# A fused decoder layer in program order on every engine: split stream, four-way decay, heads in pairs

## The chip, the cores and the metric

The kernel runs on one core of a Trainium2 chip. A core has a matrix engine (PE, TensorE), a vector engine (DVE), a scalar engine (ACT), a general engine (POOL) and a queue that issues transfers (SP); each runs its own instructions in order and waits on semaphores for the others. Tensors are read from HBM into on-chip memory (SBUF) by DMA; PE writes its results into PSUM, 128 partitions wide. The metric is the time of one execution in microseconds (us).

## The reference

One layer of a hybrid decoder, one sequence of 256 tokens, width 2048:

```python
h = rmsnorm(x, norm_gain[l])
z = h @ w_in[l]
(gq, gk_, gv, ggate, gdown, fq, fk, fv, flogit, fgate,
 mq, mgate, merge) = jnp.split(z, IN_OFFSETS, axis=-1)
gk_log = log_sigmoid(gdown @ w_gk_up[l] + b_gk[l]) / 16
o_a = gla_chunked(gq, gk_, gv, gk_log)      # S_t = diag(exp g_t) S_{t-1} + k_t v_t^T ; o_t = q_t S_t
o_a = rmsnorm(o_a, gla_norm_gain[l]) * silu(ggate)
log_f = log_sigmoid(flogit + b_f[l])
o_b = forgetting_attention(fq, fk, fv, log_f) * silu(fgate)   # causal, bias cumsum(log_f)
mk, mv = jnp.split(rmsnorm(mem, mem_norm_gain[l]) @ w_mem_kv[l], 2, axis=-1)
o_c = memory_attention(mq, mk, mv) * silu(mgate)
gates = sigmoid(merge.reshape(B, S, 3, D))
y = sum(gates[:, :, i] * (o_i @ wb_i) for i in range(3))
return rmsnorm(x + y @ w_out[l], final_gain)
```

Gated linear attention (GLA) has 4 heads (keys 128, values 256), the forgetting attention (fox) 8 heads of 64, the cross-attention 4 heads of 128 over 256 memory tokens. All inputs and outputs are 32-bit floats.

## The kernel before, in words

**Products.** Every wide product runs as split products: a 32-bit weight w is cast to a form that PE multiplies fast (`hi`, on ACT, L124) and the rest is kept as `lo = w - hi` (on DVE, L125). x and the memory are split likewise, with the norm's gain folded in (`split_x`; L256, L257). A product is then hi times hi, hi times lo and lo times hi. The weights come in blocks of 512 columns and 16 k-tiles ("kt", 128 rows each), as four quarters of 1 MB. A raw quarter lies in one of three `raw` buffers; it is split into two pieces of two kts, and there are four buffers each for `hi` and `lo`.

**Blocks.** A block runs either as `natural` (tokens on the partitions, weights moving: per kt and half of the tokens three 512-wide matmuls, L166 to L168) or as `transposed` (columns on the partitions, x moving: a 512-wide matmul with `hi`, which has x's hi and lo side by side, and a 256-wide one with `lo`, L187 and L189, for four groups of columns c and, after the first block, four kts at a time). In order of time: GLA queries (block 0, transposed), keys (1, transposed), values (2 and 3, natural), fox queries and keys (4 and 5, transposed), fox values (6), memory keys and values (7 and 8), memory queries (9), five gates, then four times three merge gates and one branch projection, then four output blocks.

**Side work.** The norm is applied late: sums of squares of x are taken on ACT, `rsqrt` makes `xcol`, and a matmul of ones with a diagonal of it makes `xrow` (`row_of`), by which results are scaled. A small product (L386, 16 matmuls) gives the low-rank decay input and the forget logits. The GLA decay is a running sum (L432) of log-sigmoids (L401 to L405). The scores inside a chunk of 128 are built in seven levels (block sizes 64 down to 1): per level DVE and ACT make scaled queries and keys, PE multiplies them for the eight chunk heads (64 columns each, L495), DVE multiplies by a mask (L497) and adds (L500); a diagonal term is added first (L477, L478). Fox handles a head in stages (scores L568, L569; masked maximum L571; exponents L576; normalising L580; transposes L585; values L593, L594). Side work stands in generators ("lanes"), and `pull()` runs one step of two lanes after each kt.

**What sets the order.** In this kernel PE and SP run in the order in which the program was written. DVE, ACT and POOL are ordered by the framework's scheduler; weight splits have a priority 1000 ahead of everything else. In block 0 the loads of x and weights come in small portions, interleaved with their splits.

**Names in the change.** `w_load`, `w_split`, `first_piece`: the new stream of loads and splits; `post`: a third lane for evictions; `small`, `rms_of`, `row_of`, `gla_decay`, `gla_scores`, `fox`, `memory`: the generators. In listings below a name such as `hi_264` is one tile, `raw_259<-wall` a load.

Of the kernel before, what the change touches and what calls it, by code (L numbers as in the profile page):

```python
# [51 lines left out]
AHEAD = 1000  # L52
LEVEL_GAP = 11
N_WARM = 8
LEVELS = (64, 32, 16, 8, 4, 2, 1)
# [4 lines left out]
def body(ctx, tc, xT, memT, xn, memn, wall, wsm, wup, cst, fgain, out):  # L60
# [7 lines left out]
    bpool = ctx.enter_context(tc.tile_pool(name="bpool", bufs=6))  # L68
# [4 lines left out]
    ctx.enter_context(tc.manual_schedule(engines={mybir.EngineType.PE, mybir.EngineType.SP}))  # L73
# [42 lines left out]
    main, side = Lane(), Lane()  # L116

    def pull():
        side.pull()
        main.pull()  # L120


    def split_w(src, hi, lo):
        nc.scalar.copy(hi, src)  # L124
        nc.vector.tensor_tensor(out=lo, in0=src, in1=hi.bitcast(F32), op=ALU.subtract)  # L125

    def w_quarter(i, q):
        raw = wpool.tile([P, 4, NB], F32, tag="raw", name=nm("raw"), bufs=3)
        nc.sync.dma_start(raw, wall[i, :, 4 * q:4 * q + 4, :])
        res = []  # L130
        for s in range(2):
            hi = wpool.tile([P, 2, NB], F32R, tag="hi", name=nm("hi"))
            lo = wpool.tile([P, 2, NB], F32R, tag="lo", name=nm("lo"))
            split_w(raw[:, 2 * s:2 * s + 2, :], hi, lo)
            res.append((hi, lo))
        return res
# [8 lines left out]
    def w_kts(i):  # L145

        for kt in range(KT):
            if kt % 4 == 0:
                with tc.high_priority(AHEAD):
                    res = w_quarter(i, kt // 4)  # L150
            hi, lo = res[(kt % 4) // 2]
            yield kt, hi[:, kt % 2, :], lo[:, kt % 2, :]
# [19 lines left out]
    def transposed(h, wsrc, bank=acc, group=4):  # L172
# [4 lines left out]
        ps = [bank() for _ in range(4)]  # L177
        held = []
        for item in wsrc:
# [3 lines left out]
            for c in range(4):  # L183
                cs_ = slice(c * P, (c + 1) * P)
                for kt, hi, lo in held:
                    hk = h_of(h, kt)
                    MM(ps[c], lhsT=hi[:, cs_], rhs=hk.rearrange("p a s -> p (a s)"),  # L187
                       start=(kt == 0), stop=False, skip_group_check=True)
                    MM(ps[c][:, :S], lhsT=lo[:, cs_], rhs=hk[:, 0, :], start=False,  # L189
                       stop=(kt == KT - 1), skip_group_check=True)  # L190
                if group == 4:
                    pull()
            for _ in held if group < 4 else ():
                pull()
            held = []
        return ps


    def rsqrt(r, m4, n):
# [4 lines left out]
        nc.scalar.activation(p, p, AF.Exp, scale=-0.5)  # L204
        nc.vector.tensor_tensor(out=u, in0=p, in1=p, op=ALU.mult)
# [3 lines left out]
    def rms_of(src, col, stage):  # L209

        ssq = spool.tile([P, NT, 2], F32, tag="ssq", name=nm("ssq"))
        for t in range(NT):
            for c in range(2):
                raw = stage()
                nc.sync.dma_start(raw, src[:, t, c * 1024:(c + 1) * 1024])
                nc.scalar.activation(raw, raw, AF.Square, accum_out=ssq[:, t, c:c + 1])
                yield 2
# [3 lines left out]
        rsqrt(col, ms, NT)  # L221
        yield 3

    def row_of(col, row):
# [4 lines left out]
        yield 3  # L229
        ps = att()  # L230
        MM(ps[:, :S], lhsT=ones, rhs=dg.rearrange("p t s -> p (t s)"), start=True, stop=True)
        nc.scalar.copy(row, ps[:, :S])
# [20 lines left out]
    x12 = []  # L253
# [5 lines left out]

    def load_split(src, tag, gcol, g, h, raw, ks):  # L260

        nc.sync.dma_start(raw[:, ks, :], src[:, 4 * g + ks.start:4 * g + ks.stop, :])
        for k in range(ks.start, ks.stop):
            kt = 4 * g + k
            split_x(h, raw[:, k, :], k, cs[:, gcol + kt:gcol + kt + 1])
# [6 lines left out]
    def load_mem():  # L272
        for g in range(4):
            m12.append(new_h("m12_", g))
            raw = wpool.tile([P, 4, S], F32, tag="raw", name=nm("raw"), bufs=3)
            load_split(memT, "m12_", C_MGAIN, g, m12[g], raw, slice(0, 4))
            yield 6

    def first_w():

        wb = w_block()
        for g in range(4):
            raw = wpool.tile([P, 4, NB], F32, tag="raw", name=nm("raw"), bufs=3)
            xraw = a4([P, 4, S])
            h = new_h("x12_", g)
            x12.append(h)
            step = 1 if g < 2 else 2
            for s in range(2):
                with tc.high_priority(AHEAD):
                    hi = wpool.tile([P, 2, NB], F32R, tag="hi", name=nm("hi"))  # L290
                    lo = wpool.tile([P, 2, NB], F32R, tag="lo", name=nm("lo"))
                    for k in range(0, 2, step):
                        ks = slice(2 * s + k, 2 * s + k + step)
                        load_split(xT, "x12_", C_GAIN, g, h, xraw, ks)
                        cut = (0, 256, NB) if g == 0 and ks.start == 0 else (0, NB)
                        for a, b in zip(cut, cut[1:]):
                            nc.sync.dma_start(raw[:, ks, a:b], wall[wb, :, 4 * g + ks.start:4 * g + ks.stop, a:b])
                            split_w(raw[:, ks, a:b], hi[:, k:k + step, a:b], lo[:, k:k + step, a:b])
                for k in range(2):
                    yield 4 * g + 2 * s + k, hi[:, k, :], lo[:, k, :]  # L300
# [8 lines left out]
    def plain_T(ps):  # L309

        r = a4([P, 4, S])
        for c in range(4):
            nc.scalar.copy(r[:, c, :], ps[c][:, S:])
            nc.vector.tensor_tensor(out=r[:, c, :], in0=ps[c][:, :S], in1=r[:, c, :], op=ALU.add)
        return r

    def scale_T(r, row):
        nc.vector.tensor_tensor(out=r, in0=r, in1=row.unsqueeze(1).to_broadcast([P, 4, S]), op=ALU.mult)
        return r

    def evac_T(ps, row):
        return scale_T(plain_T(ps), row)

    def evac_N(ps, col):
        r = a4([P, NT, NB])
        for t in range(NT):
            nc.scalar.activation(r[:, t, :], ps[t], AF.Copy, scale=col[:, t:t + 1])  # L327
        return r

    def proj_T():  # L330
        return evac_T(transposed(x12, w_kts(w_block())), xrow)

    def proj_N():
        return evac_N(natural(x12, range(KT), w_kts(w_block())), xcol)

    G["q"] = plain_T(transposed(x12, first_w(), att, 1))


    wsr = cpool.tile([P, KT, 24], F32, name="wsr")
    nc.sync.dma_start(wsr, wsm)  # L340
    wup_s = cpool.tile([16, 512], F32, name="wup_s")
    nc.sync.dma_start(wup_s, wup)

    gmask = cpool.tile([P, len(LEVELS), 64], F32, name="gmask")
    nc.gpsimd.memset(gmask, QS)
    for li, s in enumerate(LEVELS):
        nb = 64 // s
        mk_ = gmask[:, li, :].rearrange("p (b s) -> p b s", s=s)
        nc.gpsimd.affine_select(out=mk_, in_=mk_, pattern=[[-2 * s, nb], [0, s]],
                                compare_op=ALU.is_ge, fill=0.0, base=0, channel_multiplier=1)  # L350
        nc.gpsimd.affine_select(out=mk_, in_=mk_, pattern=[[2 * s, nb], [0, s]],
                                compare_op=ALU.is_ge, fill=0.0, base=s - 1, channel_multiplier=-1)
    gdiag = cpool.tile([P, P], F32, name="gdiag")
    nc.vector.tensor_scalar(gdiag, ident, QS, None, ALU.mult)

    fmask = cpool.tile([P, 3 * P], F32, name="fmask")
    nc.gpsimd.memset(fmask, 0.0)
    for c in (0, 2):
        nc.gpsimd.affine_select(out=fmask[:, c * P:(c + 1) * P], in_=fmask[:, c * P:(c + 1) * P],
                                pattern=[[-1, P]], compare_op=ALU.is_ge, fill=-1e30,  # L360
                                base=0, channel_multiplier=1)


    zs = []
    for g in range(2):
        z0 = a4([P, 8, P], F32)
        nc.gpsimd.memset(z0, 0.0)
        ws = a4([P, 8, P], F32R)
        wr = wsr[:, 8 * g:8 * g + 8, :]
        nc.vector.tensor_copy(ws, z0)  # L370
        for (a, b, wdt) in ((0, 0, 16), (32, 16, 8)):
            nc.vector.tensor_copy(ws[:, :, a:a + wdt], wr[:, :, b:b + wdt])
            nc.vector.tensor_tensor(out=ws[:, :, 64 + a:64 + a + wdt], in0=wr[:, :, b:b + wdt],
                                    in1=ws[:, :, a:a + wdt].bitcast(F32), op=ALU.subtract)
        zs.append(ws)
    sm = cpool.tile([64, S], F32, name="sm")

    def small_and_norm():

        yield 5  # L380
        norm = rms_of(xn, xcol, lambda: a4([P, 1024]))
        for _ in range(4):
            yield next(norm)
        sp = att()
        for kt in range(KT):
            MM(sp, lhsT=zs[kt // 8][:, kt % 8, :], rhs=h_of(x12, kt).rearrange("p a s -> p (a s)"),  # L386
               start=(kt == 0), stop=(kt == KT - 1))
# [541 lines left out]
```

## Time and profile before

| | |
|---|---|
| time, median of 3 runs | 824.92 us (824.08 to 825.22) |
| profiled execution, its own time | 824.89 us |
| its span, first to last instruction | 823.2 us |
| PE busy, DVE, ACT, POOL | 809.6, 497.6, 408.4, 15.4 us |
| mean granted clock of PE | 0.997 |
| bytes read from HBM | 154.39 MB |
| last matmul ends, execution ends | 814 us, 823 us |

Busy time of an engine is the sum of its instructions; matmuls are pipelined, so a row's duration is longer than the time between two starts, and the time that a matmul holds PE is read as the difference of two start times. In rows of groups the last numbers are the count, the busy time with the mean in ns of one, and the idle time just before the group with what ended it. In rows of time they are start, duration and what ran, with the idle time before it and its releaser in brackets.

### The profile page before, as it was taken

The page shows a single profiled execution, that of the slowest core. Times are in us where ns is not written, and L with a number is a line of the kernel's source. Part 1 is how long each engine was busy: PE and PEld are TensorE (multiplying, and loading weights), DVE is VectorE, ACT ScalarE, POOL GpSimd, SP SyncE. Part 2 cuts the span into 40 slices and gives each one's busy share as a digit, 9 for nine tenths or more (in the row PEclk, how much of TensorE's full clock was granted, in tenths as well). Part 3 has the DMA queues.
Part 4 walks back from the last instruction along what each step waited for, and adds up shares of the span by engine and source line. Part 5 has one row for each costly group of instructions (what it writes and reads, how often), then busy time and mean ns, then how long its engine had stood idle before and what let it go on. Part 6 is the DMA issues. An engine that isn't in the chain of part 4 may idle for free.

```text
span 823.2 us, 10033 instructions
## 1 busy us (share of the span) xinstructions
PE 809.6 (98%) x3958; PEld 679.4 (83%) x3958; DVE 497.6 (60%) x657; ACT 408.4 (50%) x547; POOL 15.4 (2%) x36
## 2 busy tenths in 40 slices
PE   8999999999999999999999999999999999999995
PEld 7888888888888778888888888888888888888885
DVE  6755988875647667567445744475446544566833
ACT  7746755743454456455444444444444444445611
POOL 4000100000000000000000000000000000000000
PEclk9999999999999999999999999999999999999998
DMA  8943466844534344445555545554555455576803
GB/s 302 385 176 125 155 228 230 300 158 169 189 140 168 108 148 154 148 160 199 182 187 199 205 170 192 200 204 167 191 205 202 166 195 205 199 266 249 307 0 103
DMA packets 27359, 157.15 MB, mean 191 GB/s; under 512 B 3216, under 2 KB 4640, under 8 KB 10416
## 3 DMA queue, kind: packets, MB, share of 16 engines
q1 hardware_dynamic: 27040, 156.48, 53.3%
q8 instruction: 31, 0.51, 0.2%
q14 instruction: 16, 0.13, 0.0%
q10 hardware_dynamic: 144, 0.02, 0.0%
q0 software_dynamic: 128, 0.02, 0.0%
HBM read 154.39 MB, written 2.10 MB: 190 GB/s over the span
## 4 chain that ended last, share of the span: by engine, by line
PE 90%; DVE 3%; DMA 2%; ACT 2%; issue 1%; SPq 1%; POOL 0%; DVEq 0%; ACTq 0%; POOLq 0%
PE acc L166 18%; PE acc L168 18%; PE acc L167 18%; PE acc L187 12%; PE acc L189 6%; PE acc L822 4%; PE acc L821 4%; PE acc L820 4%; DMA raw<-wall 1%; PE att L495 1%; DMA raw<-memT 1%; PE att L187 1%; DVE lo L125 1%; ACT hi L124 1%; PE att L593 1%
## 5 line engine op out<-in xcount | busy, mean ns | idle before, releaser
L125 DVE TENSOR_TENSOR lo<-raw,hi 128x1024 fp32r<-128x1024 f32 (+2 forms) x269 | 321.0, 1203 | 248.4 <-ACT hi L124 248.0
L124 ACT CAST hi<-raw 128x1024 fp32r<-128x1024 f32 (+2 forms) x269 | 275.3, 1035 | 291.1 <-PE acc L168 215.2
L166 PE MATMUL acc<-hi,x 128*128 128x512 f32 x544 | 215.3, 396 | 0.0
L168 PE MATMUL acc<-hi,x 128*128 128x512 f32 x544 | 212.0, 390 | 0.0
L167 PE MATMUL acc<-lo,x 128*128 128x512 f32 x544 | 211.8, 389 | 0.0
L187 PE MATMUL acc<-x,hi 128*128 128x512 f32 x384 | 137.2, 400 | 1.1 <-ACT a L327 1.1
L168 PEld LDWEIGHTS acc<-hi,x 128*128 128x128 f32 x544 | 102.1, 188 | 21.7
L166 PEld LDWEIGHTS acc<-hi,x 128*128 128x128 f32 x544 | 102.2, 188 | 21.2 <-issue 0.5
L167 PEld LDWEIGHTS acc<-lo,x 128*128 128x128 f32 x544 | 102.2, 188 | 20.5
L189 PE MATMUL acc<-x,lo 128*128 128x256 f32 x384 | 107.3, 280 | 0.0
L187 PEld LDWEIGHTS acc<-x,hi 128*128 128x128 f32 x384 | 72.1, 188 | 18.1 <-ACT a L327 1.6
L189 PEld LDWEIGHTS acc<-x,lo 128*128 128x128 f32 x384 | 72.4, 189 | 0.3
L166 PE MATMUL acc<-hi,oT 128*128 128x512 f32 x128 | 49.8, 389 | 0.0
L167 PE MATMUL acc<-lo,oT 128*128 128x512 f32 x128 | 49.8, 389 | 0.0
L168 PE MATMUL acc<-hi,oT 128*128 128x512 f32 x128 | 49.8, 389 | 0.0
L820 PE MATMUL acc<-hi,a 128*128 128x512 f32 x96 | 37.5, 391 | 0.0
L822 PE MATMUL acc<-hi,a 128*128 128x512 f32 x96 | 37.4, 389 | 0.0
L821 PE MATMUL acc<-lo,a 128*128 128x512 f32 x96 | 37.4, 389 | 0.0
L167 PEld LDWEIGHTS acc<-lo,oT 128*128 128x128 f32 x128 | 24.0, 188 | 5.0
L168 PEld LDWEIGHTS acc<-hi,oT 128*128 128x128 f32 x128 | 24.0, 188 | 5.0
L166 PEld LDWEIGHTS acc<-hi,oT 128*128 128x128 f32 x128 | 24.0, 188 | 5.0
L187 PE MATMUL att<-x,hi 128*128 128x512 f32 x64 | 23.4, 406 | 0.5 <-ACT hi L124 0.5
(215 smaller groups left out, 781.3 us busy)
## 6 DMA issues: line engine op xcount, KB each, us to landing
raw<-wall SPq DMA_DIRECT2D x132, 1024.0 KB, 4.7
a<-xn SPq DMA_DIRECT2D x8, 512.0 KB, 8.5
raw<-wall SPq DMA_DIRECT2D x4, 512.0 KB, 7.2
raw<-memT SPq DMA_DIRECT2D x4, 512.0 KB, 4.2
raw<-memn SPq DMA_DIRECT2D x4, 512.0 KB, 4.6
out<-a SPq DMA_DIRECT2D x8, 256.0 KB, 3.3
raw<-wall SPq DMA_DIRECT2D x7, 256.0 KB, 4.9
a<-xT SPq DMA_DIRECT2D x8, 128.0 KB, 4.2
```

What stands on the lines that cost most here:

```text
L124: nc.scalar.copy(hi, src)
L125: nc.vector.tensor_tensor(out=lo, in0=src, in1=hi.bitcast(F32), op=ALU.subtract)
L166: MM(ps[t], lhsT=h1, rhs=hi, start=(kt == first), stop=False)
L167: MM(ps[t], lhsT=h1, rhs=lo, start=False, stop=False)
L168: MM(ps[t], lhsT=h2, rhs=hi, start=False, stop=(kt == last))
L187: MM(ps[c], lhsT=hi[:, cs_], rhs=hk.rearrange("p a s -> p (a s)"), start=(kt == 0), stop=False, skip_group_check=True)
L189: MM(ps[c][:, :S], lhsT=lo[:, cs_], rhs=hk[:, 0, :], start=False, stop=(kt == KT - 1), skip_group_check=True)
L495: MM(ps[:, e, :], lhsT=E[:, e * P:(e + 1) * P], rhs=Q[:, e, :], start=True, stop=True)
L593: MM(o, lhsT=fv[:, 0, hs], rhs=pt[:, :S], start=True, stop=False, skip_group_check=True)
L820: MM(ps, lhsT=h1, rhs=hi, start=(kt == 0), stop=False)
L821: MM(ps, lhsT=h1, rhs=lo, start=False, stop=False)
L822: MM(ps, lhsT=h2, rhs=hi, start=False, stop=(kt == KT - 1))
```

## The change

1. All five engines now run in program order. What the scheduler decided on DVE, ACT and POOL is now where the generators stand.
2. The weights become one stream over all blocks but the last: `w_split(n)` splits piece n, `w_load` loads its quarter, and a block asks for pieces three ahead of the one it multiplies (`AHEAD = 3`). From the fourth quarter on `w_load` is asked for two quarters ahead. Block 0's pieces, which also load and split x, are made by `first_piece`.
3. Evictions (`join`, `proj_N`, gates) are steps of the lane `post`, and chains such as `rsqrt`, `log_sigmoid` and the silu gates have more `yield`s, that is, kts between their steps.
4. The small product (now L366) runs in three parts during block 0 and block 1; the memory's loads are staged in other buffers than `raw`, and the norms of x and memory load two halves at a time.
5. GLA scores: levels of 64 to 1 become three four-way levels (32, 8, 2; a block of 4s tokens against its three earlier quarters, 192 columns a matmul) and a level for pairs with the diagonal. Scores are copied under a mask into `gA` (`copy_predicated`, L636) in place of multiply and add. The term between the two chunks of 128 (L485 before, L582 now) is as it was.
6. Fox heads go in pairs, with the value matmuls of the two heads in turn on the two halves of the PSUM partitions. Memory heads are staged one step apart.
7. Warm-up matmuls 8 to 7; the small tiles' pool 6 to 8 buffers.

```diff
-AHEAD = 1000
+AHEAD = 3
+N_WARM = 7
+STEPS = (32, 8, 2)
-    ctx.enter_context(tc.manual_schedule(engines={mybir.EngineType.PE, mybir.EngineType.SP}))
+    ctx.enter_context(tc.manual_schedule())
...
     def pull():
+        post.pull()
         side.pull()
         main.pull()
...
+    def w_load(upto):
+        while done[0] <= min(upto, 4 * N_STREAM - 1):
+            i, q = divmod(done[0], 4)
+            raws[done[0]] = wpool.tile([P, 4, NB], F32, tag="raw", name=nm("raw"), bufs=3)
+            if i:
+                nc.sync.dma_start(raws[done[0]], wall[i, :, 4 * q:4 * q + 4, :])
+            done[0] += 1
+    def w_split(upto):
+        while done[1] <= min(upto, 8 * N_STREAM - 1):
+            n = done[1]
+            q, s = divmod(n, 2)
+            w_load(q + (2 if q >= 3 else 0))
+            hi = wpool.tile([P, 2, NB], F32R, tag="hi", name=nm("hi"))
+            lo = wpool.tile([P, 2, NB], F32R, tag="lo", name=nm("lo"))
+            if q < 4:
+                first_piece(q, s, raws[q], hi, lo)
+            else:
+                split_w(raws[q][:, 2 * s:2 * s + 2, :], hi, lo)
+            parts[n] = (hi, lo)
+            done[1] += 1
...
+    def small():
...
+        yield 2
+        nc.sync.dma_start(wsr, wsm)
+        nc.sync.dma_start(wup_s, wup)
+        yield 5
+        for g in range(2):
+            ws, wr = zs[g], wsr[:, 8 * g:8 * g + 8, :]
+            for (a, b, wdt) in ((0, 0, 16), (32, 16, 8)):
+                nc.vector.tensor_copy(ws[:, :, a:a + wdt], wr[:, :, b:b + wdt])
+                nc.vector.tensor_tensor(out=ws[:, :, 64 + a:64 + a + wdt], in0=wr[:, :, b:b + wdt],
+                                        in1=ws[:, :, a:a + wdt].bitcast(F32), op=ALU.subtract)
+            yield 1
+        sp = acc()
+        for kts, n in ((range(0, 8), 3), (range(8, 12), 4), (range(12, 16), 1)):
+            for kt in kts:
+                MM(sp, lhsT=zs[kt // 8][:, kt % 8, :], rhs=h_of(x12, kt).rearrange("p a s -> p (a s)"),
+                   start=(kt == 0), stop=(kt == KT - 1))
+            yield n
...
+            for c in range(4):
+                ps = att()[:, :2 * Q_N].rearrange("p (a b) -> p a b", a=2)
+                for j in range(2):
+                    e = 2 * c + j
+                    MM(ps[:, j, :], lhsT=E[:, e * P:(e + 1) * P], rhs=Qs[c // 2][:, e % 4, :],
+                       start=True, stop=True)
...
+                yield 1
+                for dst, mask, src in places:
+                    nc.vector.copy_predicated(
+                        dst, mask.bitcast(U32).unsqueeze(1).to_broadcast(list(src.shape)), src)
...
+        def values(p):
+            po = att()
+            for a, b, j, sl in ((0, S, 0, slice(0, S)), (P, S, 1, slice(S, 3 * P))):
+                for e in range(2):
+                    h = 2 * p + e
+                    MM(po[64 * e:64 * e + 64, a:b], lhsT=fv[:, j, h * 64:(h + 1) * 64], rhs=pts[h][:, sl],
+                       start=(j == 0), stop=(j == 1), skip_group_check=True)
+            return po
```

Three places show how the instructions moved. First the loads on SP in block 0: `xT` and `wall` into an `a` and a `raw` tile are x and weights, `wsr` and `wup_s` the small weights. Before, the loads of block 0's last quarter (`raw_291`) and the first of block 1 (`raw_406`, `raw_448`):

```order
L262 DMA a_237<-xT 128x512
L297 DMA raw_236<-wall 128x1024
L262 DMA a_292<-xT 128x512
L297 DMA raw_291<-wall 128x1024
L340 DMA wsr<-wsm 128x384
L342 DMA wup_s<-wup 16x512
L129 DMA raw_406<-wall 128x2048
L129 DMA raw_448<-wall 128x2048
```

and now, where the last quarter of block 0 is `raw_259` and block 1 begins with `raw_260` and `raw_262`:

```order
L353 DMA wsr<-wsm 128x384
L354 DMA wup_s<-wup 16x512
L328 DMA a_205<-xT 128x512
L331 DMA raw_202<-wall 128x1024
L144 DMA raw_260<-wall 128x2048
L144 DMA raw_262<-wall 128x2048
L328 DMA a_266<-xT 128x512
L331 DMA raw_259<-wall 128x1024
```

Block 1's two quarters moved ahead of block 0's last one, and the small weights ahead of its third one's second half.

Second, DVE in the same stretch, in the changed kernel: L300 and L132 are the splits of x and weights, L359 and L360 make the split small weights.

```order
L132 TENSOR_TENSOR lo_234<-raw_202,hi_233 128x1024
L300 SCALAR_TENSOR_TENSOR x_38_267<-a_266,cs,x_38_267 128x256 x2
L132 TENSOR_TENSOR lo_265<-raw_259,hi_264 128x1024
L359 CAST a_188<-wsr 128x8x16
L360 TENSOR_TENSOR a_188<-wsr,a_188 128x8x16
L359 CAST a_188<-wsr 128x8x8
L360 TENSOR_TENSOR a_188<-wsr,a_188 128x8x8
```

On PE the first eight small matmuls, which read `a_188`, now stand between kt 9 and kt 10 of block 0:

```order
L215 MATMUL att_183<-x_29_206,hi_203 128x512
L217 MATMUL att_183<-x_29_206,lo_204 128x256
L366 MATMUL acc_326<-x_7_113,a_188 128x512 x4
L366 MATMUL acc_326<-x_14_147,a_188 128x512 x4
L215 MATMUL att_174<-x_29_206,hi_233 128x512
```

Before, the 16 small matmuls stood together late in block 1, and the small weights were split on DVE when block 0 had ended.

Third, DVE around `xcol` (L244 to L246) and the diagonal for PE's L273, at the turn from block 1 to block 2, in the changed kernel:

```order
L132 TENSOR_TENSOR lo_648<-raw_539,hi_647 128x1024
L132 TENSOR_TENSOR lo_652<-raw_539,hi_651 128x1024
L300 SCALAR_TENSOR_TENSOR m_72_573<-a_574,cs,m_72_573 128x256
L244 TENSOR_TENSOR nwu_626<-nwp_625 128x2
L245 SCALAR_TENSOR_TENSOR nwu_626<-nwu_626,ms_622 128x2
L246 SCALAR_TENSOR_TENSOR xcol<-nwu_626,nwp_625 128x2
L270 TENSOR_SCALAR b_666<-ident,xcol 128x128 x2
```

In before the scheduler had put this chain among block 1's splits. On ACT the steps of the log-sigmoid (L457 to L462), the memory's splits (L299) and the weight casts (L131) stand in this order in block 2, up to the exponents of the cross-chunk term (L574, L575), which PE's L582 uses:

```order
L131 CAST hi_785<-raw_681 128x1024
L299 ACTIVATE m_94_702<-a_703,cs 128x256
L462 ACT_TABLE_LOAD
L462 ACTIVATE a_725<-a_725 128x1024
L462 ACTIVATE fc<-fc 8x256
L299 ACTIVATE m_94_702<-a_703,cs 128x256
L131 CAST hi_807<-raw_681 128x1024
L131 CAST hi_832<-raw_730 128x1024
L131 CAST hi_853<-raw_730 128x1024
L413 ACTIVATE a_850<-acc_643,xcol 128x512
L299 ACTIVATE m_113_817<-a_818,cs 128x256
L574 ACT_TABLE_LOAD
```

The casts of the weight stream stand in one queue with the chain's steps, where a priority had put them ahead before.

More of the change, by code (lines that the diff above doesn't have):

```diff
@@ L170, in natural, with transposed @@
         return ps
-    def transposed(h, wsrc, bank=acc, group=4):
-        ps = [bank() for _ in range(4)]
+    def transposed(h, wsrc, evac, bank=acc, group=4):
+        ps = [None] * 4
         held = []
@@ L195, in transposed, with last @@
             held = []
-        return ps
+        if group < 4:
+            for c in range(3):
+                evac(c, ps[c])
+        def last():
+            yield 1
+            evac(3, ps[3])
+        post.append(last())
     def rsqrt(r, m4, n):
@@ L274, in load_mem @@
             m12.append(new_h("m12_", g))
[L275 to L300, printed above, removed]
@@ L336, in body @@
[L336 to L352, printed above, removed]
@@ L376, in body @@
[L376 to L387, printed above, removed]
-        yield from norm
+        transposed(h, w_kts(w_block(), 2), join(r))
+        for t in then:
+            post.append(t(r))
@@ new lines, in proj_T, with scaled, then, proj_N @@
+        return r
+    def scaled(row, by=1.0):
+        def then(r):
+            yield 1
+            scale_T(r, row, by)
+        return then
+    def proj_N(h, col):
+        ps = natural(h, range(KT), w_kts(w_block()))
+        r = a4([P, NT, NB])
+        def evac():
+            for t in range(NT):
+                yield 1
+                nc.scalar.activation(r[:, t, :], ps[t], AF.Copy, scale=col[:, t:t + 1])
+        post.append(evac())
+        return r
+    gmask = cpool.tile([P, len(STEPS), Q_N], F32, name="gmask")
@@ new lines, in fox @@
+        for k in range(6):
+            this, last = (2 * k, 2 * k + 1), (2 * k - 2, 2 * k - 1)
+            if k >= 2:
+                po = values(k - 2)
+                yield 1
+                nc.scalar.copy(ob[:, k - 2, :], po[:, :S])
+            if 1 <= k < 5:
+                for h in last:
+                    trans(h)
+                yield 1
+                for h in last:
+                    moved(h)
+            if k < 4:
+                for h in this:
+                    scores(h)
+                yield 1
+                for h in this:
+                    masked(h)
+                yield 1
+                for h in this:
+                    exps(h)
+                yield 2
+                for h in this:
+                    normed(h)
+                yield 1
@@ L692, in body @@
+    side.append(small())
+    gq = G["q"] = a4([P, 4, S])
+    transposed(x12, w_kts(w_block()), join(gq), att, 1)
+    make_masks()
+    main.append(scale_first())
+    side.append(gap(8))
+    side.append(load_mem())
+    side.append(rms_of(memn, mcol, lambda: a4([P, 1024])))
+    side.append(row_of(mcol, mrow))
+    G["k"] = proj_T(x12)
     main.append(gla_decay())
     main.append(gla_scores())
-    gv = [proj_N()]
-    gv.append(proj_N())
+    gv = [proj_N(x12, xcol)]
+    gv.append(proj_N(x12, xcol))
```

613 lines of the change are left out of this document (357 added, 256 removed).

## The prediction

> **What bounds the kernel now.** I read the page first: its span and the busy time of each engine.
>
> ```profile
> span 823.2 us, 10033 instructions
> PE 809.6 (98%) x3958; PEld 679.4 (83%) x3958; DVE 497.6 (60%) x657; ACT 408.4 (50%) x547; POOL 15.4 (2%) x36
> ```
>
> PE works for 809.6 of 823.2 us. The profiled execution took 824.89 us, 1.7 us more than its span, and lies on the median of the three runs (824.92), so I add to 824.9. Next, the waits of PE, and the splits (forms, then count | busy, mean ns | idle before it and what ended that):
>
> ```profile
> PE acc L187 <- ACT a L327: 1.1, 1, 1.1
> PE att L612 <- ACT b L616: 0.7, 1, 0.7
> L124 ACT CAST hi<-raw 128x1024 fp32r<-128x1024 f32 x260 | 270.1, 1051 | 288.5 <-PE acc L168 215.2 <-issue 25.6 <-PE acc L822 21.7
> L125 DVE TENSOR_TENSOR lo<-raw,hi 128x1024 fp32r<-128x1024 f32 x260 | 315.4, 1223 | 246.0 <-ACT hi L124 245.9
> ```
>
> The casts wait for PE to free a hi tile (215.2 us): splits stand ready and PE almost never waits. So the change can gain only PE's own work and the few gaps, about 10 us, whereas any instruction that reaches PE before its operand costs its full delay.
>
> **Part 1, the start: the order of loads.** In the new SP queue both 1 MB quarters of block 1 (raw_260, raw_262) stand ahead of block 0's last loads, and raw_262 takes the tile that the split lo_234 frees. On DVE the split of x's small weights (L359, L360) stands behind lo_265, which needs one of those last loads; on PE the small projections (L366) stand behind kt 9. Rows of before at that place, PE, ACT, DVE, SP (start, us):
>
> ```profile
> 21.28 0.39 PE L187 MATMUL att<-x,hi 128*128 128x512 f32 x1
> 21.63 0.39 PE L187 MATMUL att<-x,hi 128*128 128x512 f32 x1
> 18.55 1.05 ACT L124 CAST hi<-raw 128x1024 fp32r<-128x1024 f32 x1
> 20.51 1.05 ACT L124 CAST hi<-raw 128x1024 fp32r<-128x1024 f32 x1
> 22.59 1.05 ACT L124 CAST hi<-raw 128x1024 fp32r<-128x1024 f32 x1 [0.22 <-DMA raw<-wall]
> 26.41 2.00 ACT L124 CAST hi<-raw 128x1024 fp32r<-128x1024 f32 x2 [2.77 <-DMA raw<-wall]
> 19.63 1.23 DVE L125 TENSOR_TENSOR lo<-raw,hi 128x1024 fp32r<-128x1024 f32 x1
> 34.83 0.33 DVE L372 CAST a<-wsr 128x128 fp32r<-128x128 f32 x2
> 35.09 0.43 DVE L373 TENSOR_TENSOR a<-wsr,a 128x128 fp32r<-128x128 f32 x2
> 17.22 3.98 SPq L129 DMA_DIRECT2D raw<-wall  x2
> 49.36 3.83 PE L386 MATMUL att<-x,a 128*128 128x512 f32 x16
> ```
>
> A transposed pair takes 0.35 us, a kt of four pairs 1.38; kt 10 starts at 21.63. Pieces land 2.0 us apart (casts at 18.55, 20.51, 22.59: 512 KB of weights and 256 KB of x each), and the first quarter (1 MB) about 3.8 us after the last of them with the small loads between: 0.3 to 0.4 MB a us. Now raw_260 follows the landing at 18.5 (to about 21.3), raw_262 is issued when lo_234 ends (19.63 + 1.23 = 20.9) and lands at about 24, then the piece of 0.75 MB at about 26.0. Cast 1.05, lo 1.2, L359/L360 0.7: 29.0. PE is ready for L366 at 21.6: **+7.4** (6.6 to 8.0, landing 25.2 to 26.6). Nothing behind it on PE can pass, and the loads of block 1 that came early save nothing, since before never waited for them. The 16 small matmuls are only moved (0).
>
> A PE that idles this long may come back slowly. The rows of the start:
>
> ```profile
> 1.13 3.78 PE L251 MATMUL att<-ones 128*128 128x128 f32 x16 [1.13 <-DVE ones L243]
> 5.35 0.63 PE L187 MATMUL att<-x,hi 128*128 128x512 f32 x1
> 5.78 0.41 PE L189 MATMUL att<-x,lo 128*128 128x256 f32 x1
> 6.39 0.39 PE L187 MATMUL att<-x,hi 128*128 128x512 f32 x1
> 6.62 0.28 PE L189 MATMUL att<-x,lo 128*128 128x256 f32 x1
> ```
>
> A 512-wide matmul holds PE for 0.43 us at 5.35 and for 0.23 at 6.39, after 5.3 us of work. No gap of this trace tells whether it falls back, so 0 to 2.6 (half of 5.3); I take the middle, **+1.3**. The Trainium skill ("TensorE: Matmul & The Clock Gate", Part 1) says that one idle window of about 3.4 us halves the clock until a window of work has passed; by it this term would be an estimated 1.7, and the start's rows agree with its two speeds.
>
> **Part 2, three chains that are now queued in program order.** Durations:
>
> ```profile
> L216 ACT ACTIVATE a<-a 128x1024 f32<-128x1024 f32 x4 | 4.2, 1052 | 0.0
> L204 ACT ACT_TABLE_LOAD x3 | 3.8, 1283 | 0.1
> L313 ACT COPY a<-acc 128x256 f32<-128x256 f32 x28 | 10.1, 368 | 14.2 <-PE acc L189 14.0 <-issue 0.2
> L256 ACT ACTIVATE m<-raw,cs 128x256 fp32r<-128x256 f32 x16 | 6.9, 498 | 8.8 <-DMA raw<-memT 8.8
> L432 DVE TENSOR_TENSOR_SCAN a<-a,a 128x1024 f32<-128x1024 f32 x1 | 2.3, 2291 | 0.1
> 41.18 0.16 DVE L205 TENSOR_TENSOR nwu<-nwp 128x2 f32<-128x2 f32 x1 [1.79 <-ACT nwp L204]
> 41.77 0.48 DVE L228 TENSOR_SCALAR b<-ident,xcol 128x128 f32<-128x128 f32 x2
> 61.35 0.60 PE L231 MATMUL att<-b,ones 128*128 128x256 f32 x2
> 60.21 0.39 PE L167 MATMUL acc<-lo,x 128*128 128x512 f32 x1
> 60.44 0.39 PE L168 MATMUL acc<-hi,x 128*128 128x512 f32 x1
> ```
>
> (a) xcol. In before its diagonal was ready at 42.3 and PE used it at 61.35. Now L273 stands 12 matmuls into block 2 (12 x 0.227 = 2.7 us after block 1 ends). Count from that end. ACT is held by PE to the start of block 1's last group (-5.5): two casts 2.1, two squares 2.1, copy 0.4, table load 1.3, two tiny ones 0.4, copy, m piece, copy 1.2, two casts 2.1, m piece 0.4 end at +4.5. DVE then: second lo until 5.2, m piece 0.45, three tiny ones 0.6, diagonal 0.5: 6.7. Stall **+4.0** (2.5 to 4.9).
>
> (b) The cross-chunk matmul L582 stands six kts (8.2 us) into block 3. Count from its start. The cast hi_756 is held by PE until -10.9; behind it ACT has, in order, four more casts (4.2), four m pieces (L299) at 0.45, six log-sigmoid steps (three of 1.05, three small of 0.4) and one table load: the log-sigmoid's Ln ends at -1.8, the fourth cast, hi_853, at 1.8. DVE: lo_808 0.9, L465 2.4, the scan 4.7, lo 5.9, short scan and negation 6.7, lo 7.9, L571 8.5. ACT: two Exps 9.8, cast 10.8. DVE: lo 12.0, two m pieces 12.8, L577 and L578 (512 wide, 0.6 each) 14.0. Stall **+5.8** (3 to 7).
>
> (c) mcol. L273 for the memory stands directly behind block 4. Count from its end: ACT's L593 waits for DVE's two lo's and L528 until -6.7; then L593 1.05, two squares 2.1, L597 0.85, two casts 2.1, table load, Ln, table load, Exp 2.9, copy 0.4 end at 2.7; DVE's add, three tiny ones and the diagonal end at 4.2. Stall **+4.2** (3 to 4.7).
>
> In before each of these was covered by hundreds of matmuls; cover gone, the delay is paid whole. The pairs of heads and memory have shorter steps of this kind, each on the other side of one or two kts (1.36 us of PE): eight rounds at 0 to 0.6 us give 0 to 5, and since most of their steps are one or two splits long (1.2 us each) I take **+2.0**. The copies under a mask (44 on DVE) have no row; the nearest is the add's 1.2 ns an element (L125): three of them, 384 elements, take 0.5 us, at twice the price 1.0, both less than the kt between two uses, so they lie in these 0 to 5.
>
> **Part 3, what PE saves.**
>
> ```profile
> 117.91 1.89 PE L495 MATMUL att<-b,a 128*128 128x64 f32 x16
> 119.61 0.48 PE L187 MATMUL acc<-x,hi 128*128 128x512 f32 x1
> 73.47 1.05 PE L477 MATMUL att<-a,a 128*128 128x128 f32 x8
> 74.28 0.48 PE L166 MATMUL acc<-hi,x 128*128 128x512 f32 x1
> 337.79 1.03 PE L634 MATMUL att<-b,a 128*128 128x256 f32 x4
> 338.66 0.60 PE L626 MATMUL att<-ident,b 128*128 128x128 f32 x4
> 261.58 0.65 PE L593 MATMUL att<-b,a 128*64 128x256 f32 x2
> 262.37 0.55 PE L585 MATMUL att<-ident,b 128*128 128x128 f32 x3
> ```
>
> A level held PE for 1.70 us (117.91 to 119.61), seven 11.9, the diagonal twice 0.81: 13.5. Now 32 matmuls 192 wide, two passes each (16 records were 8 matmuls before); a pass is between 0.10 (128 wide) and 0.22 (256 wide), 0.16: 10.2. **-3.3.** Values of a fox head held PE 0.79, eight 6.3, plus 0.1 of entry each; in pairs on two column halves, one behind the other 6.0 in all, side by side 3.4: 1.1 to 3.7, I take **-2.0**. The gaps around L327 and L616 go (two waits above, 2.4 with the slow starts beside them): **-2.4**, 0 if they return in another place. The tail is in the same order: 0. So is one warm-up matmul less, since L187 first waits for ACT.
>
> Sum: 7.4 + 1.3 + 4.0 + 5.8 + 4.2 + 2.0 = 24.7; 24.7 - 7.7 = +17.0: **842**. With the low ends of the losses (15.1) and high ends of the gains (9.4) 831, the other way round 852.
>
> **Rivals.** *Chains in time* (not slower): ACT and DVE, 50% and 60% busy, run so far ahead that (a) to (c) and the later steps cost nothing, because ACT's order lets casts wait less for PE than I count. For it: casts idle 288 us before. Against it: that idle time is the wait for PE itself, and what is queued behind such a cast waits too. It leaves 7.4 - 7.7: 824.6, and 823 with the heads fully side by side; it decides once the three chains together cost less than 2 us. *Start harmless*: the last piece lands as before, and PE waits 1.9 us for L360 (22.8 + 0.7 against 21.6). Against it: one queue, served in order, in which casts follow landings. 842 - 7.4 - 1.3 + 1.9 = 835. *Cold after every stall*: each of (a) to (c) idles 4 to 6 us and each brings up to 2.6 more, about 1.7 in the middle: 842 + 5 = 847, up to 853. For it: half speed until 6 us; against: a pause of 4 us is shorter than any that the rows show as cold. The same section of that page of the Trainium skill would have it so; nothing in this trace idles long enough to agree or not.
>
> **Chances.** Sum as forecast 0.58 (831 to 852), chains in time 0.16, start harmless 0.08, both of these (about 817) 0.04, cold after every stall 0.14. A difference under 0.2% (1.6 us) can't be told from none here. Faster: both, and half of chains in time: 0.12. Same: 0.05. Slower: 0.83. The range reaches down to chains in time and up to the cold case's middle: 824 to 851.
>
> **What would show it.** PE idle of 6.6 to 8.0 us before L366 ended by DVE L360, with ACT's cast for kt 12 ended by a DMA at about 26; matmuls behind it at 0.43 or 0.23 us; PE waits at L273 (two times 4 us, ended by DVE L270) and at L582 (6 us, by DVE L578); a level of eight L622 at 2.6 us. No stall at L582 and L273 would prove the order of ACT and DVE harmless, and a PE busy time above 809 the saving wrong.

## The result

The changed kernel takes 845.36 us (843.13 to 846.40), before 824.63 us (824.08 to 825.22): 1.0248 times as long, 95% interval 1.0224 to 1.0271. Forecast were 842 us, slower, and a range of 824 to 851.

The page of the changed kernel, first the span and the busy time of the engines:

```profile
span 844.6 us, 9971 instructions
PE 811.8 (96%) x3892; PEld 678.3 (80%) x3892; DVE 500.7 (59%) x700; ACT 404.3 (48%) x551; POOL 22.1 (3%) x44
```

PE is busy about as long as before (811.8 against 809.6 us), in a span that is 21.4 us longer. Most of that time is in waits. All waits of PE in the changed kernel (who waited on whom: us in total, times, longest):

```profile
PE acc L366 <- DVE a L360: 8.7, 1, 8.7
PE att L582 <- DVE a L578: 5.5, 1, 5.5
PE att L273 <- DVE b L270: 3.5, 2, 2.6
PE att L778 <- DVE b L791: 1.2, 1, 1.2
PE att L734 <- DVE b L726: 1.2, 1, 1.2
PE att L294 <- DVE ones L286: 1.1, 1, 1.1
PE att L217 <- DVE lo L132: 1.0, 3, 0.6
PE acc L191 <- DVE a L385: 0.5, 1, 0.5
PE acc L192 <- DVE lo L132: 0.3, 1, 0.3
```

Before, five short waits were all there was. Now three places that the prediction named (L366, L582, L273 twice) hold 17.7 us, and the heads (L734, L778) 2.4.

The first of them in the rows of the changed kernel, PE, ACT and DVE (start, us, what, and the idle time before it with its releaser):

```profile
21.08 0.28 PE L217 MATMUL att<-x,lo 128*128 128x256 f32 x1
30.06 3.75 PE L366 MATMUL acc<-x,a 128*128 128x512 f32 x8 [8.70 <-DVE a L360]
33.61 0.63 PE L215 MATMUL att<-x,hi 128*128 128x512 f32 x1
25.45 0.91 ACT L299 ACTIVATE x<-a,cs 128x256 fp32r<-128x256 f32 x2 [5.35 <-DMA a<-xT]
26.79 1.04 ACT L131 CAST hi<-raw 128x1024 fp32r<-128x1024 f32 x1 [0.43 <-DMA raw<-wall]
27.87 1.22 DVE L132 TENSOR_TENSOR lo<-raw,hi 128x1024 fp32r<-128x1024 f32 x1 [0.99 <-ACT hi L131]
29.69 0.23 DVE L360 TENSOR_TENSOR a<-wsr,a 128x64 fp32r<-128x64 f32 x1
```

The late piece lands at 26.8, is cast and split until 29.1, and only then come the small weights that PE has waited for since 21.4. The eight small matmuls then take 3.55 us from their start to the next one, 0.44 each; before, sixteen took 3.67, 0.23 each. The granted clock beside it (windows of the changed kernel: length, then busy us of PE, PEld, DVE, ACT, POOL, then the clock, DMA share, GB/s):

```profile
30.00:40.00 10.00, 9.94 (x38) 8.26 (x39) 4.96 (x9) 1.73 (x2) 0.00 (x0) 0.72 0.30 106
40.00:67.00 27.00, 27.00 (x154) 23.35 (x153) 12.48 (x17) 14.84 (x24) 0.96 (x1) 1.00 0.77 267
112.00:130.00 18.00, 18.00 (x74) 14.98 (x74) 13.45 (x21) 9.69 (x14) 0.00 (x0) 0.85 0.47 162
```

It was 0.72 in the ten microseconds behind the first wait and 0.85 in the eighteen behind L582, where before shows full clock. PE counts as busy while its matmuls run at half speed, so part of the longer span is hidden in its busy time.

### The profile page after: what moved, and what is told of

Read it like the earlier page. It is cut to its first block, busy times and chain, and to the rows that moved or that the text cites. A ratio compares the mean times of both kernels' runs of the same rounds, so it can differ in the third digit from the quotient of the medians.

```text
span 844.6 us, 9971 instructions
## 1 busy us (share of the span) xinstructions
PE 811.8 (96%) x3892; PEld 678.3 (80%) x3892; DVE 500.7 (59%) x700; ACT 404.3 (48%) x551; POOL 22.1 (3%) x44
## 4 chain that ended last, share of the span: by engine, by line
PE 65%; DVE 1%; ACT 0%; DVEq 0%; issue 0%; ACTq 0%
PE acc L193 15%; PE acc L192 15%; PE acc L191 15%; PE acc L215 4%; PE acc L1012 3%; PE acc L1011 3%; PE acc L1013 3%; PE acc L217 2%; PE att L778 0%; PE att L922 0%; PE att L796 0%; PE att L822 0%; PE att L734 0%; PE att L787 0%; DVE lo L132 0%; ACT hi L131 0%
## 5 line engine op out<-in xcount | busy, mean ns | idle before, releaser
L132 DVE TENSOR_TENSOR lo<-raw,hi 128x1024 fp32r<-128x1024 f32 (+2 forms) x269 | 322.0, 1207 | 275.6 <-ACT hi L131 275.0
L131 ACT CAST hi<-raw 128x1024 fp32r<-128x1024 f32 (+2 forms) x269 | 275.1, 1035 | 317.4 <-PE acc L193 240.2
```

Of the source, the lines that this page charges most:

```text
L131: cast(hi, src)
```

## The experiments

All but one start from the changed kernel, whose 845.4 us is the figure to compare with; before took 824.0 to 825.1 us beside each of them.

**Loads in order.** Block 0's last loads stand ahead of block 1's quarters again.

```diff
-            w_load(q + (2 if q >= 3 else 0))
+            w_load(q + (2 if q >= 4 else 0))
```

> The changed kernel, with block 0's last loads ahead of block 1's two quarters on SP again; DVE and PE orders as changed. Theory (the order of the loads makes the first stall): the last pieces land near 21 us instead of 26.7, PE waits for L360 until about 24.1 instead of 30.1, so 2.9 us instead of 8.9, and nothing behind it runs at half speed (2.4 us): 845.4 - 6.0 - 2.4 = 837. Rival (the place of the small weights' split in DVE's queue makes it, wherever the loads stand): the wait stays above 7 us, 844 to 846.

Measured: 836.97 us (835.09 to 839.95), ratio to before 1.0139 [1.0122, 1.0156].

```profile
PE acc L366 <- DVE a L360: 2.8, 1, 2.8
```

The wait went from 8.7 to 2.8 us and the time by 8.4: the order of the loads made the first stall. The rest of it, 2.8 us, ends with L360 too, which stands behind the split on DVE. One thing was not as expected: there is half speed behind a wait as short as this. PE in this run:

```profile
23.73 2.54 PE L366 MATMUL acc<-x,a 128*128 128x512 f32 x8 [2.79 <-DVE a L360]
26.07 0.63 PE L215 MATMUL att<-x,hi 128*128 128x512 f32 x1
28.41 0.35 PE L217 MATMUL att<-x,lo 128*128 128x256 f32 x1
28.60 0.40 PE L215 MATMUL att<-x,hi 128*128 128x512 f32 x1
```

and the clock in windows of two microseconds:

```profile
24.00:26.00 2.00, 2.00 (x8) 1.60 (x7) 1.97 (x5) 1.05 (x1) 0.00 (x0) 0.79 1.01 422
26.00:28.00 2.00, 2.00 (x8) 1.64 (x7) 1.44 (x3) 0.00 (x0) 0.00 (x0) 0.50 0.83 262
28.00:30.00 2.00, 2.00 (x11) 1.72 (x11) 0.00 (x0) 0.00 (x0) 0.00 (x0) 0.86 0.76 315
```

PE starts again at full speed, falls to half about 1.5 us later (a matmul every 0.43 us from 25.2) and is at full speed again at 28.6, 3.4 us after it fell: 1.5 us lost.

**Small matmuls later.** The first twelve small matmuls move to kt 14 and 15; the loads stay in the changed order.

```diff
+        yield 4
         sp = acc()
-        for kts, n in ((range(0, 8), 3), (range(8, 12), 4), (range(12, 16), 1)):
+        for kts, n in ((range(0, 8), 1), (range(8, 12), 2), (range(12, 16), 1)):
```

> The changed kernel with the first twelve small matmuls four kts later (kt 14 and 15), loads in the changed order. Theory (loads): PE runs kt 10 and 11 and then waits for the split of the late piece, from about 24.0 to 29.1: 5.1 us in place of 8.9, and its matmuls at half speed still follow: 845.4 - 3.8 = 841.6. Rival (DVE's queue): no wait over 1 us, 834.

Measured, one execution: 842.72 us.

```profile
PE att L215 <- ACT hi L131: 4.2, 2, 3.9
PE att L217 <- DVE lo L132: 1.1, 4, 0.5
```

PE now waits for the late piece itself, at kt 12: 3.9 us for the cast and then for the split, some 5 in all. So the loads alone stall PE, and L366's earlier place in the queue adds the rest. Both are needed to be rid of it.

**Cross term later.** L582, and the scores behind it, come five kts later.

```diff
         nc.vector.tensor_tensor(out=cd[:, :, 1, :], in0=cd[:, :, 1, :], in1=gq[:, :, P:], op=ALU.mult)
-        yield 2
+        yield 7
```

> The changed kernel with L582 and all of the scores behind it five kts (6.8 us of PE) later. Theory (PE is there too early and pays the delay whole): the 5.6 us wait at L582 is gone and so is the half speed after it (2.2 us): 845.4 - 7.8 = 837.6. Rival (the delay belongs to the queues of ACT and DVE and turns up at the next use, L622, or at the end of the attention): 843 to 846.

Measured: 838.06 us (837.14 to 839.87), ratio 1.0163 [1.0147, 1.0178]. L582 is gone from the list of waits; new in it are

```profile
PE att L722 <- DVE b L717: 1.3, 1, 1.3
PE att L622 <- DVE a L563: 0.6, 1, 0.6
```

7.3 us of the 7.8 came. A part of the chain behind it does turn up later, 1.9 us and not 5.5, and the 1.2 us at L734 are gone from the list in exchange. (The first wait was 7.6 us in this profile; in the profiles of all kernels that leave the start as it is, it lay between 7.6 and 9.5.)

**Two kts instead of five**, at the same place:

> The changed kernel with L582 two kts (2.7 us of PE) later, where five took its wait away. Theory (PE pays the delay whole, one for one): a wait of 5.5 - 2.7 = 2.8 us at L582 in place of 5.5. Rival (the chain is held by PE's own progress and moves with it): 4.5 or more. Half speed behind it: as behind the 2.8 us wait of an earlier run, 1.5 us; none if it needs a longer idle time.

Measured, one execution: 841.2 us, and

```profile
PE att L582 <- DVE a L578: 2.7, 1, 2.7
PE att L273 <- DVE b L270: 4.6, 2, 2.6
```

2.7 us of PE's work ahead of it took 2.8 from the wait: PE pays the delay one for one. The memory's L273, one of the two in the second line, grew from 0.9 to 2.0; that ACT and DVE are now two kts later there is the likely reason, not a shown one. Half speed appeared behind the wait at L582 too (108.7 to 111.7 us, some 1.4 us lost against the same matmuls at full speed) and behind the 2.0 us of the memory's L273 (clock 0.50 from 150 to 152 us).

**x's L273 later**, three kts, with all that is behind it in its lane:

```diff
-    def row_of(col, row):
+    def row_of(col, row, more=0):
...
-        yield 1
+        yield 1 + more
         ps = att()
...
-        yield from row_of(xcol, xrow)
+        yield from row_of(xcol, xrow, 3)
```

> The changed kernel with x's L273 (and the chain behind it in its lane) three kts later, 4.1 us of PE. Theory: the waits at x's L273 and beside it (3.9 us) go, and with them some half speed behind (0.8 to 1.5); L582 keeps its 5.5: 845.4 - 4.7 = 840.7. Rival (DVE and ACT are simply late by then and the wait turns up at L480 or L582, which grows to 9): 845.

Measured, one execution: 846.56 us. No gain: here the rival was right in the sum, though not in the place.

```profile
PE att L582 <- DVE a L578: 4.8, 1, 4.8
PE acc L191 <- DVE a L385: 2.3, 2, 1.8
PE att L273 <- DVE b L270: 1.8, 1, 1.8
PE att L622 <- DVE a L563: 0.7, 1, 0.7
```

x's wait (2.6 us) is gone. But moving the lane by three kts put other steps beside each other: the eviction of block 7 (L384 on ACT, L385 on DVE) now stands behind the norm of GLA's output with its two table loads (L241, L242, 1.28 us each on ACT) and holds up block 8 (1.8), the memory's L273 waits 1.8 in place of 0.9, L622 0.7. And PE falls to half speed behind the 1.8 us wait, from 234.7 to 241.5 us. A window of this run (same columns as above, clock 0.50):

```profile
236.00:240.00 4.00, 4.00 (x13) 3.25 (x13) 3.01 (x13) 0.00 (x0) 0.00 (x0) 0.50 0.47 158
```

Half of 6.8 us, an estimated 3.4, is lost there; without it the move would have gained an estimated 2 us. That L582 did not grow fits a chain that hangs on PE's progress and not on how late x's was.

**PE kept busy.** Matmuls of ones fill the two largest waits, into banks that the following matmuls overwrite.

```diff
         sp = acc()
+        for _ in range(37):
+            MM(sp[:, :P], lhsT=ones, rhs=ones, start=True, stop=True)
...
         ps = att()
+        for _ in range(22):
+            MM(ps[:, :P], lhsT=ones, rhs=ones, start=True, stop=True)
         for h in range(4):
             MM(ps[:, h * P:(h + 1) * P], lhsT=cd[:, h, 0, :], rhs=cd[:, h, 1, :], start=True, stop=True)
```

> The changed kernel with 37 matmuls of ones (7.9 us warm) ahead of L366 and 22 (4.7 us) ahead of L582, into banks that are then overwritten, so that PE works while it waits for DVE. Theory (an idle PE falls to half speed, and that costs 2.4 us behind the first stall and 2.2 behind L582): both waits end when they did, the matmuls behind them run at 0.23 us, 845.4 - 4.6 = 840.8. Rival (the slow matmuls have another cause, or work in the gap costs as much as it saves): 844.5 to 847.

Measured: 840.60 us (839.96 to 842.37), ratio 1.0194 [1.0179, 1.0209], 4.8 us less. Nothing was put earlier in the program; PE only wasn't idle. So the slow matmuls come from idle time, and at two waits they cost 4.8 us. At x's L273, which was left, the same run shows half speed after 2.6 us of waiting:

```profile
70.47 0.70 PE L273 MATMUL att<-b,ones 128*128 128x256 f32 x2 [2.59 <-DVE b L270]
72.40 0.63 PE L193 MATMUL acc<-hi,x 128*128 128x512 f32 x1
72.00:75.00 3.00, 3.00 (x9) 2.32 (x8) 2.14 (x4) 0.00 (x0) 0.00 (x0) 0.50 0.74 306
```

(the last line is a window of the same columns as above: clock 0.50).

Half speed does not follow each such wait. x's L273 waits 2.6 us in the changed kernel and in seven of the runs; the clock falls behind it in the changed kernel, with loads in order and with PE kept busy, and not in the other five. The changed kernel, where PE is slow from the first matmul on, and the run with two kts, where it is not slow at all:

```profile
73.70 1.22 PE L273 MATMUL att<-b,ones 128*128 128x256 f32 x2 [2.56 <-DVE b L270]
75.14 0.63 PE L192 MATMUL acc<-lo,x 128*128 128x512 f32 x1
```

```profile
72.03 0.70 PE L273 MATMUL att<-b,ones 128*128 128x256 f32 x2 [2.59 <-DVE b L270]
72.80 0.39 PE L192 MATMUL acc<-lo,x 128*128 128x512 f32 x1
```

The times at which the clock changes say why. In the changed kernel it is at half from 25.4 to 35.6, from 73.2 to 76.6 and from 110.7 to 117.5 us; between one of these times and the next lie 3, 11, 1, 10 and 2 times 3.41 us, and in the other traces the changes lie on such a grid too. The clock thus changes only at the ends of steps of 3.41 us that run on whatever PE does. Between the start and the last matmul, in all traces here, it fell at the end of each full-speed step in which PE had waited 1.8 us or more (20 steps), and of none in which it had waited 1.7 us or less. A wait of 2.6 us that the end of a step cuts in two can cost nothing more, and one of 1.8 us inside a step is enough.

**Fox heads, in turn or not.** First the order alone, head after head on the two column halves:

```diff
-            for a, b, j, sl in ((0, S, 0, slice(0, S)), (P, S, 1, slice(S, 3 * P))):
-                for e in range(2):
+            for e in range(2):
+                for a, b, j, sl in ((0, S, 0, slice(0, S)), (P, S, 1, slice(S, 3 * P))):
```

> The changed kernel with the value matmuls of a fox pair head after head, not in turn on the two column halves; same matmuls. If two halves run side by side, PE is held longer by the 32 value passes: 4 x (1.30 - 0.85) = 1.8 us more in the sum of the start-to-start times of L734. If they do not, the sum stays within 0.3 us. The time of one execution (845 to 848) can't tell it.

Measured, one execution: 843.97 us; L734's sum is 3.68 us against 3.66. By my expectation this speaks against side by side, but the expectation was badly made. The eight passes of a pair, as the trace has them here, start two by two (262.14 and 262.15, 262.41 and 262.42, and so on): matmuls ran side by side although the program names the heads one after the other; in which order they reached PE the trace does not tell. So the run could not separate the two, and the next one puts both heads on the same half:

```diff
-                    MM(po[64 * e:64 * e + 64, a:b], lhsT=fv[:, j, h * 64:(h + 1) * 64], rhs=pts[h][:, sl],
+                    MM(po[0:64, e * S + a:e * S + b], lhsT=fv[:, j, h * 64:(h + 1) * 64], rhs=pts[h][:, sl],
...
-                nc.scalar.copy(ob[:, k - 2, :], po[:, :S])
+                for e in range(2):
+                    nc.scalar.copy(ob[64 * e:64 * e + 64, k - 2, :], po[0:64, e * S:e * S + S])
```

> The changed kernel with the values of both heads of a fox pair on the same half of PSUM's partitions (64 columns of the array), one head beside the other in the bank, and two copies on ACT to bring them apart. Theory (two halves run side by side, whatever their order in the program): from the first L734 of a pair to the next matmul 1.4 to 1.7 us in place of 0.8. Rival (pairs are cheap because PE enters and leaves the narrow form half as often): 0.8 to 0.95. The time of one execution, 845 to 849, is told apart only by the trace.

(The fox values of this form are not the reference's; the number of matmuls and their sizes are as in the others.) Measured, one execution: 849.32 us. A pair in the changed kernel, then on one half:

```profile
264.42 0.87 PE L734 MATMUL att<-b,a 128*64 128x256 f32 x8
265.22 0.50 PE L215 MATMUL acc<-x,hi 128*128 128x512 f32 x1
```

```profile
263.29 1.51 PE L734 MATMUL att<-b,a 128*64 128x256 f32 x8
264.73 0.50 PE L215 MATMUL acc<-x,hi 128*128 128x512 f32 x1
```

From the start to the next matmul 0.80 us against 1.44: the two halves do run side by side. Over the four pairs the sum of L734 is 5.81 us against 3.66 (the last pair of the changed kernel takes 1.26), so that is worth 2.1 us.

**All four waits taken away.** Loads in order, small matmuls later, L582 five kts later (as above), x's L273 three and the memory's one kt later.

```diff
-        yield from row_of(xcol, xrow)
+        yield from row_of(xcol, xrow, 3)
...
-    side.append(row_of(mcol, mrow))
+    side.append(row_of(mcol, mrow, 1))
```

> The changed kernel with block 0's loads ahead of block 1's, the small matmuls at kt 14 and 15, x's L273 three kts later, the memory's one kt later, L582 five kts later. Theory (the slowdown is these four waits and the half speed behind them, and the savings on PE are real): 845.4 - 8.9 - 5.2 - 3.9 - 5.6 - 1.1 = 820.7, faster than before by 0.3 to 0.6%, with up to 2 us of new waits at the fox heads. Rival (program order on DVE and ACT only moves the waits on to the next use): 830 or more.

Measured: 820.00 us (819.14 to 821.12), ratio to before 0.9937 [0.9918, 0.9957]: 0.6% faster than before, 25.4 us faster than the changed kernel. PE's busy time and its longest waits:

```profile
PE 804.6 (98%) x3892; PEld 674.4 (82%) x3892; DVE 500.1 (61%) x700; ACT 404.5 (49%) x551; POOL 21.8 (3%) x44
PE att L735 <- DVE b L727: 1.2, 1, 1.2
PE att L294 <- DVE ones L286: 1.1, 1, 1.1
PE att L217 <- DVE lo L132: 0.7, 2, 0.5
PE acc L191 <- DVE a L386: 0.5, 1, 0.5
```

None is longer than 1.2 us, and the clock is full up to the last matmul. The step that gained nothing alone (x's) does no harm here: with five kts more at L582 the table loads of GLA's output norm come behind the last eviction of block 7. The slowdown was these waits and what follows them; program order on DVE and ACT is not slow as such.

**The last fox pair two kts later** on top of that:

```diff
                 for h in last:
                     moved(h)
+                if k == 4:
+                    yield 2
```

> The kernel with all four waits taken away, and two kts more between the transposes of the last fox pair and its values (L735, 1.3 us of wait there). Theory: that wait goes and nothing moves with it, since nothing is queued behind it that another engine needs soon: 820.0 - 1.3 = 818.7, 0.7% faster than before. Rival (memory attention, two kts later, meets a wait of its own): 820 to 821.

Measured: 819.57 us (818.59 to 821.12), ratio 0.9937 [0.9923, 0.9951]. The wait at L735 is gone from the list, but 0.4 us less is within what such runs differ by, and the first block waited longer for its splits in this profile. Whether the 1.2 us arrived is left open.

## Why the prediction was right, point by point

The sign, the mechanism and the places were right. That the sum came as near as 842 to 845.4 was in part luck: half speed was priced far too low and chain (c) far too high, and the two errors partly cancelled. The first wait (8.7) and the one of (c) (0.9) lie outside the ranges given for them, and half speed (6.2) outside its 0 to 2.6, which was meant for the first stall alone. (The upper end of the sum is 852.7, so 853 and not 852.)

| term | predicted | measured | from |
|---|---|---|---|
| loads in the wrong order, wait at L366 | +7.4 | +8.7 | list of waits |
| half speed afterwards | +1.3 | about +6.2 | 4.8 at two waits by the run with PE kept busy, 1.4 behind x's by start times |
| (a) x's L273 | +4.0 | 2.6; 3.5 with the wait on L385 ahead of it | wait; start times |
| (b) L582 | +5.8 | 5.5 | wait |
| (c) the memory's L273 | +4.2 | 0.9 | 3.5 less 2.6 |
| heads and memory | +2.0 | 2.4 | L734, L778 |
| PE's own work | -5.3 | -5.0 | PE busy 809.6 before, 804.6 with all four waits taken away |
| short waits of before | -2.4 | -1.8 | L327's and L616's are gone |

The measured column (3.5 for (a)) adds up to 20.4 us, of 20.7 between the medians and 21.4 between the spans of the two profiled executions; up to 1 us stays unattributed.

**The start.** The weights landed at 26.8 us, 0.8 later than my 26.0; the cast, the split and the four small steps of L359 and L360 behind them took 0.3 us longer than I had taken, and PE was ready at 21.4 instead of 21.6. That is the 1.3 us between 7.4 and 8.7.

**Half speed** is the term that failed: "I take the middle, +1.3". I priced it for one place, and left it out at the three chains, as a rival of its own ("Cold after every stall", 847). That rival's mechanism is what happened at two of its three chains, and the measured time lies between it and the forecast. My argument against it, that "a pause of 4 us is shorter than any that the rows show as cold", fell with the 2.6 us behind x's L273 and, in the run with x's L273 later, with 1.8 us. The trace agrees with the Trainium skill ("TensorE: Matmul & The Clock Gate", Part 1) on the two speeds and on the length of a step, which the page gives as about 3.4 us (25.2 to 28.6 with loads in order). Its rule that an idle window of that length comes first is not what these traces show: 1.8 us of waiting in a step of 3.41 were enough.

**Chain (c)** is the other. "ACT's L593 waits for DVE's two lo's and L528 until -6.7" was misread: in DVE's queue L528 stands ahead of the two lo's. ACT and DVE in the changed kernel:

```profile
141.17 1.22 DVE L528 TENSOR_TENSOR a<-a 128x1024 f32<-128x1024 f32 x1
143.36 2.36 DVE L132 TENSOR_TENSOR lo<-raw,hi 128x1024 fp32r<-128x1024 f32 x2 [0.97 <-ACT hi L131]
144.17 1.06 ACT L593 ACTIVATE a<-a 128x1024 f32<-128x1024 f32 x1
154.66 0.48 DVE L270 TENSOR_SCALAR b<-ident,mcol 128x128 f32<-128x128 f32 x2
```

L593 followed the casts at 144.2, 9.9 us before the end of block 4 (154.1) instead of 6.7. The chain ran 3.2 us earlier, and of 4.2 us there remained 0.9.

**(a) and (b)** came within 0.5 us by start times (for (a) 0.9 of the 3.5 us stood ahead of L273, where PE first waited for L385), worked out from durations and queue orders alone: six to eighteen instructions on two engines, anchored at a cast that PE itself holds back. The run with two kts fits that: PE came 2.7 us later to L582, and the wait fell from 5.5 to 2.7.

**PE's work.** The score matmuls cost 0.162 us a pass, as taken, from start to start in a row of them (0.16 was the estimate). From the levels of before to these, PE's sum of start-to-start times falls by 5.3 us (13.5 to 8.2), for the values of fox by 2.7 (6.4 to 3.7, 2.1 of it by the two halves). These sums flatter the change: behind the last pass of a group the stream's next matmul starts after 0.03 us, but it then takes longer. What I had not priced is this return: after a piece of side work the first matmul of the stream takes 0.13 us longer, and there are now 66 such returns, 51 before; that takes 2.0 us back. In all, PE's work fell by 5.0 us, as the busy time of the run with all four waits taken away shows. My own sign, "a PE busy time above 809 the saving wrong", came up in the changed kernel (811.8), but it was a bad sign, since busy time holds the matmuls at half speed too.

**Rivals.** "Chains in time" is refuted by the list of waits, "start harmless" by the 8.7 us. The copies under a mask cost 0.25 to 0.45 us each on DVE; the three of a level take 0.95 us for 192, 128 and 64 elements, which the 1.0 us at twice the price bounds, and no wait of PE ends with one.

## What to carry to other kernels

When an engine's order is written out by hand, the work of the critical engine counts less than where each of its instructions stands: work out for each hand-over when the operand is ready, by adding durations along the queues from the last point at which the critical engine itself holds them, and place the use behind that. Loads need the same: two prefetches of 1 MB for the next block, written ahead of the current block's last loads, made PE wait 5.9 us longer here. Allow behind each stall of PE that can fill half a step of 3.4 us for half speed, and check after every move of a lane what now stands beside what, since a step moved alone may only pass its wait on.

## What was not expected of the hardware

- PE's clock changes only on a grid of 3.41 us. It fell at the end of a step with at least 1.8 us of waiting, and never with 1.7 or less. So the same 2.6 us wait at x's L273 cost half speed at once (changed kernel), about 1.5 us after work was back (PE kept busy), or none (two kts). After the waits of 5.5 and 8.7 us PE was slow from the first matmul on.
- The value matmuls of a fox pair on the two column halves start within 14 ns of each other, also where the program names one head's two matmuls ahead of the other's. On one half the same eight passes take 1.44 us in place of 0.80.
